# Narrower score and value matmuls in the second block's three attentions

## The chip, the cores and the metric

The kernel runs on one core of one Trainium2 chip. The metric is the device time of one execution in microseconds (us). The engines are TensorE (PE, with its weight loads shown apart as PEld), VectorE (DVE), ScalarE (ACT), GpSimd (POOL) and SyncE (SP, which here only issues DMAs). Each engine runs its own instructions in a fixed order and waits on semaphores for the others.

## The reference

Two transformer blocks of two layers each run one after the other on 256 tokens of 1024 channels, all in fp32. The change touches the second block only, in its token mixer. There a layer has three attentions of 8 heads of 64 channels each, all causal:

```
_swa_sink: dist = i - j;  band = 0 <= dist < 128;  softmax over [logits + bias, sink];  p @ v
_fox:      logits = q.k * scale + c[i] - c[j];     masked where j > i;  softmax;  p @ v
_nsa:      p_c over 15 compressed keys, p_s over selected blocks, p_w over a window, each with
           its own masked softmax; out = g0 * p_c @ vc + g1 * p_s @ v_sel + g2 * p_w @ vw
merged = g_a * (o_a @ w_br_a) + g_b * (o_b @ w_br_b) + g_c * (o_c @ w_br_c);   out = merged @ w_out
```

With 256 tokens in two query tiles of 128, queries 0 to 127 see only keys 0 to 127; queries 128 to 255 see all 256 keys. So of the four (query tile, key tile) squares of a head one is masked as a whole.

## The kernel before, in words

**Numbers.** Every fp32 operand of a matmul is split into two fp32r parts, hi and lo: ScalarE copies hi (`split`, L536; for weights L354), VectorE subtracts to get lo (L537; for weights L356). A product is then three matmuls, hi*hi, hi*lo and lo*hi (`mm3`, L547 to L549). Weights stream from HBM in chunks of 128x1024; each chunk needs one L354 and one L356, and in the projections with 512 columns it feeds 12 matmuls of 512 columns.

**The mixer** is `mix`, called once per layer of the second block. It has three attention phases in a row, each over 8 units (a unit is one head): phase b (`simple` with `prep_b`), phase c (`simple` with `prep_c`, which adds a third score matmul, L1689, for the forget gate), and phase a (the last loop, L1874 on, with compressed, selected and window scores). A unit does this:

- scores on PE: per query tile two matmuls of one q tile against the hi and lo parts of the keys (L1685, L1686; in phase a L1847 for compressed and selected keys together, 32 + 256 columns, and L1851 for the window). In phase b and c both query tiles write into one PSUM bank at columns 0 and 128, 256 columns each, so the second overwrites what the first left of its masked half;
- bias, mask and row minimum on DVE (L625), exponentials on ACT (L615; L1863 in phase a), reciprocal and scaling on DVE (L616, L621; L1868, L1872 in phase a). These read 128 columns for the first query tile and 256 for the second;
- transposes of the three unmasked probability squares on PE (L1710; L1883 and L1884 in phase a), and the split of the 384 columns on ACT and DVE (L536, L537) into the buffers `pts`. Each of these has 512 columns: 128 of zeros, written once per layer (L1652), and behind them the three squares, A (second queries, second keys), B (first queries, first keys) and C (second queries, first keys);
- values on PE: for each of two key tiles one `mm3` of 256 columns. The first key tile reads B and C, the second reads the zeros and A. Phase a does this for selected and window keys and adds one matmul for the compressed keys (L1904).

**What fills in.** Between a unit's steps the code calls `fill(ns)`, which takes pieces of other work from a queue: projections of 512 columns (`natural`), the compression of the keys and, in phase c and a, the gates and branch products of the attention before (`branch_job`). These pieces are `mm3`s of 512 columns, each with its share of weight splits L354 and L356 and of evacuations (L1770, L1787, L1789).

**What sets the order.** When the program is built, a scheduler puts the recorded operations of each engine into one fixed sequence by their priority and by its own estimate of when each can run. Weight splits are moved in priority by `PREP` (L353). Buffers come from two arenas by best fit, so the size of one buffer can move others.

Of the kernel before, what the change touches and what calls it, by code (L numbers as in the profile page):

```python
# [18 lines left out]
P = 128  # L19
D = 1024  # L20
KT = D // P
S = 256
# [456 lines left out]
class Kern:  # L479
# [979 lines left out]
    def mix(self, l, xh, xl, mid):  # L1459
        nc, fa, ra, d = self.nc, self.fa, self.ra, self.d  # L1460
        V, A, G, PE = nc.vector, nc.scalar, nc.gpsimd, nc.tensor
# [17 lines left out]
        def parts(n):  # L1479
            b = ra.alloc(4 * n)  # L1480
            v = b.v("p (z t c) -> p z t c", z=2, t=2)
            return b, v[:, 0], v[:, 1]
# [3 lines left out]
        vswb, vsh, vsl = parts(256)  # L1486
# [22 lines left out]
        pick = pickb.a  # L1509
# [135 lines left out]
        self.push(fill_job())  # L1645

        sr = Ring(fa, 448, 3)
        pts = []
        for i in range(2):
            b = (ra.alloc(512), ra.alloc(512))  # L1650
            for z in b:
                V.tensor_copy(z.a[:, 0:P], self.zero[:, 0:P])  # L1652
            pts.append(b)
        qr = Ring(ra, S, 4)

        def pair_rows(src, c):
# [10 lines left out]
        def pair_out(og, bank, j):  # L1667
            h, lo = og
            c = slice(j * S, j * S + S)
            for k, r in enumerate((slice(0, 64), slice(64, 128))):  # L1670
                self.split(bank[r, k * S:k * S + S], h[r, c], lo[r, c])

        def simple(prep, vh, vl, paired, og, extra):

            units = [(j, i) for j in range(4) for i in range(2)]
            heads = {0: prep(0)}
            prob = {}

            def soft(u):
                j, i = u  # L1680
                q, (kh, kl), b, sink, h = heads[j][i]
                bank = self.ps.next()
                for qt in range(2):
                    qq, o = q[:, qt * P:qt * P + P], bank[:, qt * P:qt * P + S]
                    PE.matmul(o, qq, kh, start=True, stop=False)  # L1685
                    PE.matmul(o, qq, kl, start=False, stop=extra is None)  # L1686
                    if extra:
                        n = P if qt == 0 else S
                        PE.matmul(bank[:, qt * P:qt * P + n], pick[:, h:h + 1].to_broadcast([P, P]), extra[:, 0:n],  # L1689
                                  start=False, stop=True)  # L1690
                sb, ss = sr.next(), self.sm.next()
                w = 0 if sink is None else 1
                for qt in range(2):
                    n = P if qt == 0 else S
                    s = sb[:, 132 * qt:132 * qt + n + 1]
                    m, r = ss[:, 2 * qt:2 * qt + 1], ss[:, 2 * qt + 1:2 * qt + 2]
                    if w:
                        G.tensor_copy(s[:, n:n + 1], sink)
                    self.neg_add_min(s[:, :n], bank[:, qt * P:qt * P + n], b[:, S - n:], sink if w else BIG, m)
                    self.soft_tail(s, n, m, r, n + w)  # L1700
                prob[u] = sb

            for n, u in enumerate(units):
                if n == 0:
                    soft(u)
                j, i = u
                sb = prob.pop(u)
                bank = self.pt.next()
                for k, o in enumerate((132 + P, 0, 132)):
                    PE.transpose(bank[:, k * P:k * P + P], sb[:, o:o + P], ident)  # L1710
                p_h, p_l = pts[n % 2]
                self.split(bank[:, 0:384], p_h.a[:, P:], p_l.a[:, P:])
                if i == 0 and j < 3:
                    heads[j + 1] = prep(j + 1)
                if n + 1 < 8:
                    soft(units[n + 1])
                self.fill(1300)
                if i == 0:
                    self.obank = self.po.next()
                c = slice(j * P, j * P + P) if paired else slice(0, P)  # L1720
                o = self.obank[:, i * S:i * S + S]
                for kt in range(2):
                    r = slice(S - kt * S, 2 * S - kt * S)
                    self.mm3(o, vh[:, kt, c], vl[:, kt, c], p_h.a[:, r], p_l.a[:, r], kt == 0, kt == 1)
                if i == 1:
                    pair_out(og, self.obank, j)
                self.fill(700)
# [15 lines left out]

        ogb, og = new_og()
        simple(prep_b, vbh, vbl, False, og, None)
        self.flush()
        for b in (kwb, vbb, qbb, t5, gf):
# [69 lines left out]
        W1 = 288  # L1817
        slb, wib = ra.alloc(4 * W1), ra.alloc(4 * S)
        sl4 = slb.v("p (i z k) -> p i z k", i=2, z=2)
        wi4 = wib.v("p (i z k) -> p i z k", i=2, z=2)  # L1820
# [20 lines left out]
        def soft(u):  # L1841
            j, i = u
            q, hd = heads[j][i], j + 4 * i
            bs, bw = self.ps.next(), self.ps.next()
            for qt in range(2):
                for z in range(2):
                    PE.matmul(bs[:, 160 * qt:160 * qt + W1], q[:, qt * P:qt * P + P], sl4[:, i, z],  # L1847
                              start=z == 0, stop=z == 1)
            for qt in range(2):
                for z in range(2):  # L1850
                    PE.matmul(bw[:, P * qt:P * qt + S], q[:, qt * P:qt * P + P], wi4[:, i, z],  # L1851
                              start=z == 0, stop=z == 1)
            s1, s2, mm, rr = sr.next(), sr.next(), self.sm.next(), self.sm.next()
            todo = []
            for qt in range(2):
                n = P if qt == 0 else S
                for br, (dst, src, o, w, bias) in enumerate((
                        (s1, bs, 160 * qt, 32, cb4[:, qt, hd]),
                        (s1, bs, 160 * qt + 32, n, t53[:, hd, S - n:]),
                        (s2, bw, P * qt, n, t53[:, hd, S - n:]))):  # L1860
                    c = 3 * qt + br
                    self.neg_add_min(dst[:, o:o + w], src[:, o:o + w], bias, 1e20 if br == 0 else BIG, mm[:, c:c + 1])
                    A.activation(dst[:, o:o + w], dst[:, o:o + w], AF.Exp, bias=mm[:, c:c + 1], scale=-1.0,  # L1863
                                 accum_out=rr[:, c:c + 1])
                    todo.append((dst[:, o:o + w], rr[:, c:c + 1]))
            r6 = rr[:, 0:6]
            V.tensor_scalar(r6, r6, 1e-30, None, ALU.max)
            V.reciprocal(r6, r6)  # L1868
            r3 = r6.rearrange("p (t b) -> p t b", t=2)
            V.tensor_tensor(r3, r3, sg[:, :, 3 * hd:3 * hd + 3], ALU.mult)  # L1870
            for s, r in todo:
                V.tensor_scalar(s, s, r, None, ALU.mult)  # L1872
            prob[u] = (s1, s2)

        soft(units[0])
        for n, u in enumerate(units):
            j, i = u
            s1, s2 = prob.pop(u)
            pc = pcr.next()
            for k, (s, o, w) in enumerate(((s1, 160, 32), (s2, P, 0))):  # L1880
                bank = self.pt.next()
                for kk_, c in enumerate((o + w + P, w, o + w)):
                    PE.transpose(bank[:, kk_ * P:kk_ * P + P], s[:, c:c + P], ident)  # L1883
                PE.transpose(bank[0:32, 384:512], s1[:, 160 * k:160 * k + 32], ident)  # L1884
                self.split(bank[:, 0:384], pts[k][0].a[:, P:], pts[k][1].a[:, P:])
                cq, bq = slice(k * P, k * P + P), bank[0:32, 384:512]
                A.copy(pc[0:32, cq], bq)
                V.tensor_tensor(pc[32:64, cq], bq, pc[0:32, cq].bitcast(F32), ALU.subtract)
                A.copy(pc[64:96, cq], bq)
            if i == 0 and j < 3:  # L1890
                heads[j + 1] = q_pair(qa, j + 1)
            if n + 1 < 8:
                soft(units[n + 1])
            self.fill(2500)
            if i == 0:
                self.obank = self.po.next()
            o = self.obank[:, i * S:i * S + S]
            for k in range(2):
                for kt in range(2):
                    r = slice(S - kt * S, 2 * S - kt * S)  # L1900
                    c = slice(k * P, k * P + P)
                    self.mm3(o, vsh[:, kt, c], vsl[:, kt, c], pts[k][0].a[:, r], pts[k][1].a[:, r],
                             k == 0 and kt == 0, False)
            PE.matmul(o, vcmp.a, pc, start=False, stop=True)  # L1904
            if i == 1:
                pair_out(og_a, self.obank, j)
            self.fill(1000)
# [55 lines left out]
```

## Time and profile before

| what | value |
|---|---|
| time, three runs | 2344.83 us median (2343.74 to 2349.3) |
| the profiled execution | 2346.41 us; its span in the trace 2344.6 us |
| PE busy | 2261.1 us, 96% of the span, 11612 matmuls |
| DVE busy | 1696.6 us, 72% |
| ACT busy | 1249.1 us, 53% |
| mean granted TensorE clock | 0.993 of 2.4 GHz |
| matmuls of mm3, L547 to L549 | 9648 of 11612 |

A matmul's duration in the trace is longer than its share of PE's time, since matmuls overlap: the time from one start to the next is what counts. Phases b, c and a of the first layer run from about 1226 to 1259, 1296 to 1329 and 1356 to 1418 us, those of the second layer from about 1901 to 1934, 1970 to 2004 and 2031 to 2093 us.

### The profile page before, as it was taken

What the parts mean: (1) busy time and instruction counts of PE and PEld (TensorE: products, weight loads), DVE (VectorE), ACT (ScalarE), POOL (GpSimd) and SP (SyncE); (2) the same over time, 40 slices, a digit from 0 to 9 for tenths busy, and PEclk for the clock granted to TensorE, in tenths of its full rate; (3) what the DMA queues carried; (4) which work ended last, traced back from release to release, by engine and by line L of the source; (5) the groups of instructions that cost most, each with busy time, mean ns of one, the idle gap of its engine ahead of it and who ended that gap; (6) DMA issues with size and microseconds to landing.
All of it is one profiled execution on the core that took longest, in us unless ns stands there. A gap on an engine that the chain in (4) does not pass through costs nothing.

```text
span 2344.6 us, 32027 instructions
## 1 busy us (share of the span) xinstructions
PE 2261.1 (96%) x11612; PEld 1858.8 (79%) x11612; DVE 1696.6 (72%) x3192; ACT 1249.1 (53%) x2235; POOL 244.0 (10%) x265
## 2 busy tenths in 40 slices
PE   6999899999999999999999999999999999999998
PEld 3888787787778899888877777788788877777887
DVE  6598999677689997655577897755655677897554
ACT  6385673242347864444367785444444376764452
POOL 1302200222220202200000000000000000000000
PEclk9999999999999999999999999999999999999999
DMA  8121224355443335555646435556556545445554
GB/s 321 45 82 41 75 81 135 126 165 168 134 139 110 103 132 171 179 186 180 220 137 205 138 117 173 179 188 197 189 190 219 163 153 184 144 131 179 189 190 134
DMA packets 102975, 362.98 MB, mean 155 GB/s; under 512 B 11936, under 2 KB 13088, under 8 KB 102304
## 3 DMA queue, kind: packets, MB, share of 16 engines
q1 hardware_dynamic: 102816, 360.93, 46.5%
q8 instruction: 91, 1.49, 0.3%
q14 instruction: 68, 0.56, 0.1%
HBM read 359.84 MB, written 1.05 MB: 154 GB/s over the span
## 4 chain that ended last, share of the span: by engine, by line
PE 55%; DVE 8%; ACT 4%; DMA 3%; issue 2%; POOL 1%; DVEq 0%; ACTq 0%; POOLq 0%; SPq 0%
PE bank L547 17%; PE bank L549 17%; PE bank L548 16%; DVE ra_t L356 2%; ACT ra_t L354 1%; DMA fa_t<-in_gate 1%; PE bank L1402 1%; DVE ra_t L537 1%; DVE fa_t L625 1%; DVE fa_t L1339 1%; DMA fa_t<-in_n 1%; PE bank L1265 1%; ACT ra_t L536 1%; POOL fa_t L543 0%; ACT fa_t L1863 0%
## 5 line engine op out<-in xcount | busy, mean ns | idle before, releaser
L547 PE MATMUL bank<-ra_t 128*128 128x512 f32 (+1 forms) x3216 | 1186.9, 371 | 14.3 <-DVE fa_t L786 5.0
L549 PE MATMUL bank<-ra_t 128*128 128x512 f32 (+1 forms) x3216 | 1172.8, 366 | 8.3 <-DVE ra_t L537 3.8
L548 PE MATMUL bank<-ra_t 128*128 128x512 f32 (+1 forms) x3216 | 1174.6, 367 | 3.8 <-DVE ra_t L537 1.3
L356 DVE TENSOR_TENSOR ra_t<-fa_t,ra_t 128x1024 fp32r<-128x1024 f32 x583 | 722.2, 1241 | 349.1 <-ACT ra_t L354 333.6
L354 ACT CAST ra_t<-fa_t 128x1024 fp32r<-128x1024 f32 x606 | 633.2, 1048 | 602.2 <-PE bank L549 284.5
L547 PEld LDWEIGHTS bank<-ra_t 128*128 128x128 f32 x3216 | 605.4, 189 | 129.1 <-ACT ra_t L536 15.4
L549 PEld LDWEIGHTS bank<-ra_t 128*128 128x128 f32 x3216 | 605.6, 189 | 108.7 <-DVE ra_t L537 7.3
L548 PEld LDWEIGHTS bank<-ra_t 128*128 128x128 f32 x3216 | 607.2, 189 | 103.1 <-DVE ra_t L356 5.1
L865 DVE SCALAR_TENSOR_TENSOR fa_t<-fa_t 128x512 f32<-128x512 f32 (+1 forms) x240 | 161.5, 673 | 6.0 <-ACT fa_t L863 2.8
L537 DVE TENSOR_TENSOR ra_t<-bank,ra_t 128x512 fp32r<-128x512 f32 (+5 forms) x234 | 131.2, 568 | 44.0 <-ACT ra_t L536 41.1
L536 ACT CAST ra_t<-bank 128x512 fp32r<-128x512 f32 (+5 forms) x234 | 112.8, 488 | 84.8 <-PE bank L549 33.4
L543 POOL TENSOR_TENSOR fa_t<-fa_t 128x1 f32<-128x1 f32 (+2 forms) x54 | 69.0, 1278 | 762.3 <-DVE fa_t L542 762.1
L625 DVE CUSTOM_DVE_ANT_0 fa_t<-bank,fa_t 128x256 f32<-128x256 f32 (+2 forms) x320 | 117.0, 396 | 8.7 <-PE bank L1231 1.9
L615 ACT ACTIVATE fa_t<-fa_t 128x257 f32<-128x257 f32 (+5 forms) x160 | 91.5, 574 | 21.4 <-DVE fa_t L625 20.1
L1410 ACT ACTIVATE fa_t<-bank 128x256 f32<-128x256 f32 x88 | 33.9, 385 | 112.5 <-PE bank L549 112.4
L356 POOL TENSOR_TENSOR ra_t<-fa_t,ra_t 128x1024 fp32r<-128x1024 f32 x23 | 58.0, 2520 | 276.1 <-ACT ra_t L354 273.0
L1412 DVE TENSOR_TENSOR fa_t<-fa_t,bank 128x256 f32<-128x256 f32 x88 | 36.8, 418 | 65.7 <-ACT fa_t L1410 65.5
L1184 DVE SCALAR_TENSOR_TENSOR fa_t<-fa_t 128x512 f32<-128x512 f32 x98 | 71.0, 757 | 2.3 <-DMA fa_t<-in_ada 2.0
L1053 POOL TENSOR_TENSOR fa_t<-fa_t 128x512 f32<-128x512 f32 (+1 forms) x32 | 37.3, 1172 | 154.4 <-DVE fa_t L1052 154.4
L638 DVE TENSOR_TENSOR ra_t<-bank,ra_t 64x256 fp32r<-64x256 f32 (+1 forms) x96 | 43.5, 455 | 8.3 <-ACT ra_t L637 5.3
L649 POOL CAST ra_t<-fa_t 64x256 fp32r<-64x256 f32 (+3 forms) x40 | 24.0, 606 | 241.4 <-PE bank L1597 69.9
L1863 ACT ACTIVATE fa_t<-fa_t 128x32 f32<-128x32 f32 (+2 forms) x96 | 39.0, 409 | 14.5 <-DVE fa_t L625 13.9
(218 smaller groups left out, 1701.9 us busy)
## 6 DMA issues: line engine op xcount, KB each, us to landing
fa_t<-in_f1w SPq DMA_DIRECT2D x132, 512.0 KB, 4.2
fa_t<-in_f2w SPq DMA_DIRECT2D x132, 512.0 KB, 4.3
fa_t<-in_tr SPq DMA_DIRECT2D x88, 512.0 KB, 3.5
fa_t<-in_n SPq DMA_DIRECT2D x56, 512.0 KB, 3.6
fa_t<-in_ada SPq DMA_DIRECT2D x48, 512.0 KB, 4.5
fa_t<-in_gate SPq DMA_DIRECT2D x48, 512.0 KB, 3.7
fa_t<-in_nat SPq DMA_DIRECT2D x36, 512.0 KB, 4.2
fa_t<-in_proj SPq DMA_DIRECT2D x24, 512.0 KB, 3.5
```

The lines of the kernel that those rows point to most:

```text
L354: nc.scalar.copy(hi, raw)
L356: eng.tensor_tensor(lo, raw, hi.bitcast(F32), ALU.subtract)
L536: self.nc.scalar.copy(hi, src)
L537: self.nc.vector.tensor_tensor(lo, src, hi.bitcast(F32), ALU.subtract)
L543: self.nc.gpsimd.tensor_tensor(out, out, self.nhalf[:, :n], ALU.pow)
L547: mm(ps, lh, rh, start=start, stop=False)
L548: mm(ps, lh, rl, start=False, stop=False)
L549: mm(ps, ll, rh, start=False, stop=stop)
L615: nc.scalar.activation(s[:, :width or n], s[:, :width or n], AF.Exp, bias=mneg, scale=-1.0, accum_out=r)
L625: self.nc.vector.tensor_tensor_reduce(out=out, in0=a, in1=b, op0=ALU.add, op1=ALU.min, scale=-1.0, scalar=init, accum_out=acc)
L865: V.scalar_tensor_tensor(y4, src, w, y4, ALU.mult, ALU.add)
L1184: V.scalar_tensor_tensor(acc[s].a, wk, self.sc[:, kt, s:s + 1], acc[s].a, ALU.mult, ALU.add)
```

## The change

For the first query tile the score matmuls now take 128 key columns in place of 256 (160 in place of 288 in phase a). The zeros in front of the probabilities are gone: `pts` has 384 columns per buffer, the 8 fills of L1652 (4 per layer) are not there, and the values of the second key tile are made from square A alone, 128 columns, added to the second half of the output. That is 320 matmuls in both layers: 128 of scores (64 in phases b and c, 64 in phase a, of which 32 go from 288 to 160) and 192 of values (96 and 96). No matmul is added or taken away, and all that DVE and ACT read and write in a unit keeps its size.

```
-        pts = []
-        for i in range(2):
-            b = (ra.alloc(512), ra.alloc(512))
-            for z in b:
-                V.tensor_copy(z.a[:, 0:P], self.zero[:, 0:P])
-            pts.append(b)
+        pts = [(ra.alloc(3 * P), ra.alloc(3 * P)) for _ in range(2)]
...
                 for qt in range(2):
-                    qq, o = q[:, qt * P:qt * P + P], bank[:, qt * P:qt * P + S]
-                    PE.matmul(o, qq, kh, start=True, stop=False)
-                    PE.matmul(o, qq, kl, start=False, stop=extra is None)
+                    n = P if qt == 0 else S
+                    qq, o = q[:, qt * P:qt * P + P], bank[:, qt * P:qt * P + n]
+                    PE.matmul(o, qq, kh[:, :n], start=True, stop=False)
+                    PE.matmul(o, qq, kl[:, :n], start=False, stop=extra is None)
                     if extra:
-                        n = P if qt == 0 else S
-                        PE.matmul(bank[:, qt * P:qt * P + n], pick[:, h:h + 1].to_broadcast([P, P]), extra[:, 0:n],
-                                  start=False, stop=True)
+                        PE.matmul(o, pick[:, h:h + 1].to_broadcast([P, P]), extra[:, 0:n], start=False, stop=True)
...
-                self.split(bank[:, 0:384], p_h.a[:, P:], p_l.a[:, P:])
+                self.split(bank[:, 0:384], p_h.a, p_l.a)
...
-                o = self.obank[:, i * S:i * S + S]
-                for kt in range(2):
-                    r = slice(S - kt * S, 2 * S - kt * S)
+                for kt, r in enumerate((slice(P, 3 * P), slice(0, P))):
+                    o = self.obank[:, i * S + kt * P:i * S + S]
                     self.mm3(o, vh[:, kt, c], vl[:, kt, c], p_h.a[:, r], p_l.a[:, r], kt == 0, kt == 1)
...
             for qt in range(2):
+                n = P if qt == 0 else S
                 for z in range(2):
-                    PE.matmul(bs[:, 160 * qt:160 * qt + W1], q[:, qt * P:qt * P + P], sl4[:, i, z],
+                    PE.matmul(bs[:, 160 * qt:160 * qt + 32 + n], q[:, qt * P:qt * P + P], sl4[:, i, z, :32 + n],
                               start=z == 0, stop=z == 1)
...
-                    PE.matmul(bw[:, P * qt:P * qt + S], q[:, qt * P:qt * P + P], wi4[:, i, z],
+                    PE.matmul(bw[:, P * qt:P * qt + n], q[:, qt * P:qt * P + P], wi4[:, i, z, :n],
                               start=z == 0, stop=z == 1)
...
-                for kt in range(2):
-                    r = slice(S - kt * S, 2 * S - kt * S)
+                for kt, r in enumerate((slice(P, 3 * P), slice(0, P))):
                     c = slice(k * P, k * P + P)
-                    self.mm3(o, vsh[:, kt, c], vsl[:, kt, c], pts[k][0].a[:, r], pts[k][1].a[:, r],
+                    self.mm3(o[:, kt * P:], vsh[:, kt, c], vsl[:, kt, c], pts[k][0].a[:, r], pts[k][1].a[:, r],
                              k == 0 and kt == 0, False)
```

The built order changes too. It is the same as before up to the first scores of phase b and from the end of the mixer on, and the same in both layers, but inside a mixer the instructions of PE, DVE and ACT stand otherwise. In the changed kernel the lines of the mixer have numbers that are 4 to 6 lower (L1883 is L1879, L1851 is L1847, L1872 is L1868, L1770 is L1764, L1710 is L1705).

On PE in phase a, before, this is what stands between the window scores of the third unit (L1851) and the transposes of the second (L1883); the rows of bank_65 are fill:

```order
L1851 MATMUL bank_67<-ra_t 128x256 x4
L548 MATMUL bank_65<-ra_t 128x512
L549 MATMUL bank_65<-ra_t 128x512
L547 MATMUL bank_65<-ra_t 128x512
L548 MATMUL bank_65<-ra_t 128x512
L549 MATMUL bank_65<-ra_t 128x512
L547 MATMUL bank_65<-ra_t 128x512
L548 MATMUL bank_65<-ra_t 128x512
L549 MATMUL bank_65<-ra_t 128x512
L547 MATMUL bank_65<-ra_t 128x512
L548 MATMUL bank_65<-ra_t 128x512
L1883 MATMUL bank_68<-fa_t 128x128 x3
```

Now, with L1842 and L1847 for the scores and L1879 for the transposes:

```order
L1842 MATMUL bank_66<-ra_t 128x160 x2
L1842 MATMUL bank_66<-ra_t 128x288 x2
L1847 MATMUL bank_67<-ra_t 128x128 x2
L1879 MATMUL bank_68<-fa_t 128x128 x3
L1880 MATMUL bank_68<-fa_t 32x128
L1847 MATMUL bank_67<-ra_t 128x256
L1879 MATMUL bank_69<-fa_t 128x128 x3
```

The ten matmuls of fill are no longer ahead of these transposes. Counted from the transposes of the first unit to those of the last, phase a has 137 matmuls of 512 columns before and 94 now; phase c has 77 and 60, phase b 66 and 46. What is taken out stands between the phases now (101 and 114 from b to c, 97 and 121 from c to a) or behind the last unit.

On DVE in phase a, before, the rows ahead of the scaling (L1872) of the second unit:

```order
L1888 TENSOR_TENSOR ra_t<-bank_69,ra_t 32x128
L356 TENSOR_TENSOR ra_t<-fa_t,ra_t 128x1024
L1888 TENSOR_TENSOR ra_t<-bank_68,ra_t 32x128
L1867 TENSOR_SCALAR fa_t<-fa_t 128x6
L638 TENSOR_TENSOR ra_t<-bank_69,ra_t 64x256
L1868 RECIPROCAL fa_t<-fa_t 128x6
L1770 TENSOR_TENSOR fa_t<-bank_64,fa_t 128x512
L1870 TENSOR_TENSOR fa_t<-fa_t 128x6
L356 TENSOR_TENSOR ra_t<-fa_t,ra_t 128x1024
L638 TENSOR_TENSOR ra_t<-bank_69,ra_t 64x256
L1872 TENSOR_SCALAR fa_t<-fa_t 128x32
```

Now, with L1884 for L1888 and L1863 to L1868 for L1867 to L1872:

```order
L1884 TENSOR_TENSOR ra_t<-bank_69,ra_t 32x128
L1884 TENSOR_TENSOR ra_t<-bank_68,ra_t 32x128
L625 ISA fa_t<-bank_67,fa_t 128x256
L625 ISA fa_t 128x1
L356 TENSOR_TENSOR ra_t<-fa_t,ra_t 128x1024
L638 TENSOR_TENSOR ra_t<-bank_69,ra_t 64x256
L1863 TENSOR_SCALAR fa_t<-fa_t 128x6
L1864 RECIPROCAL fa_t<-fa_t 128x6
L1866 TENSOR_TENSOR fa_t<-fa_t 128x6
L1868 TENSOR_SCALAR fa_t<-fa_t 128x32
```

One weight split (L356) and one evacuation of fill (L1770) have moved out of this place. Over the same stretch of phase a as above, L356 stands there 12 times before and 9 times now and the evacuation L1789 (now L1783) 4 and 2 times; in phase c L356 6 and 4, L1770 3 and 2 and L625 28 and 26 times, L638 11 and 12; in phase b L356 9 and 7 times. All else of DVE is as often there as before.

## Rows read from the trace of the kernel before

**Rows 1.** The page, part 1: busy time of each engine, share of span.

```profile
PE 2261.1 (96%) x11612; PEld 1858.8 (79%) x11612; DVE 1696.6 (72%) x3192; ACT 1249.1 (53%) x2235; POOL 244.0 (10%) x265
```

**Rows 2.** Busy time by stretch: b, c, between, a; a of layer 1.

```profile
core 0: us, PE busy (x) PEld busy (x) DVE busy (x) ACT busy (x) POOL busy (x), PEclk, DMA share, GB/s
1226.30:1259.30 33.00, 31.86 (x189) 25.77 (x189) 28.89 (x88) 27.33 (x64) 2.70 (x9) 1.00 0.45 146
...
1295.90:1329.50 33.60, 32.69 (x186) 25.83 (x187) 30.90 (x100) 26.01 (x68) 1.86 (x5) 1.00 0.35 113
1329.50:1356.40 26.90, 26.48 (x130) 21.36 (x130) 17.95 (x48) 16.85 (x44) 0.00 (x0) 1.00 0.48 157
1356.40:1418.20 61.80, 59.09 (x339) 47.93 (x338) 58.34 (x199) 46.38 (x145) 6.15 (x4) 1.00 0.37 120
...
2030.90:2092.80 61.90, 59.15 (x340) 48.05 (x339) 58.40 (x199) 46.45 (x146) 6.16 (x4) 1.00 0.38 120
```

**Rows 3.** The chain of waits in phase a: start us, us, what.

```profile
1363.22 1.13 DVE ra_t L356
1364.83 1.30 DVE fa_t L1872 x6
...
1374.62 0.69 DVE fa_t L1872 x3
1375.35 0.55 PE bank L1883 x3
```

**Rows 4.** PE's waits in the first mixer: us in total, times, longest.

```profile
PE bank L1883 <- DVE fa_t L1872: 2.2, 3, 0.9
```

**Rows 5.** Timeline of PE, scores to transposes of phase a: start, us.

```profile
1362.48 0.73 PE L1847 MATMUL bank<-ra_t 128*128 128x288 f32 x4
1363.05 0.63 PE L1851 MATMUL bank<-ra_t 128*128 128x256 f32 x4
1363.52 0.40 PE L548 MATMUL bank<-ra_t 128*128 128x512 f32 x1
...
1365.56 0.39 PE L548 MATMUL bank<-ra_t 128*128 128x512 f32 x1
1365.92 0.55 PE L1883 MATMUL bank<-fa_t 128*128 128x128 f32 x3
```

**Rows 6.** Timeline of PE, scores of one unit of phase c.

```profile
1291.74 0.28 PE L1686 MATMUL bank<-ra_t 128*128 128x256 f32 x1
1291.86 0.22 PE L1689 MATMUL bank<-ra_t 128*128 128x128 f32 x1
1291.92 0.33 PE L1685 MATMUL bank<-ra_t 128*128 128x256 f32 x1
1292.09 0.28 PE L1686 MATMUL bank<-ra_t 128*128 128x256 f32 x1
1292.21 0.28 PE L1689 MATMUL bank<-ra_t 128*128 128x256 f32 x1
1292.32 0.40 PE L548 MATMUL bank<-ra_t 128*128 128x512 f32 x1
```

**Rows 7.** Timeline of the weight loads, the same place.

```profile
1291.74 0.19 PEld L1689 LDWEIGHTS bank<-ra_t 128*128 128x128 f32 x1
1291.86 0.19 PEld L1685 LDWEIGHTS bank<-ra_t 128*128 128x128 f32 x1
1291.97 0.19 PEld L1686 LDWEIGHTS bank<-ra_t 128*128 128x128 f32 x1
```

**Rows 8.** DVE groups in phase a: busy us, mean ns, idle before.

```profile
L356 DVE TENSOR_TENSOR ra_t<-fa_t,ra_t 128x1024 fp32r<-128x1024 f32 x12 | 15.6, 1300 | 0.1
...
L625 DVE CUSTOM_DVE_ANT_0 fa_t<-bank,fa_t 128x128 f32<-128x128 f32 x13 | 3.7, 288 | 0.9 <-PE bank L1884 0.8
...
L1789 DVE SCALAR_TENSOR_TENSOR fa_t<-fa_t,bank 128x512 f32<-128x512 f32 x4 | 2.7, 683 | 0.1
```

**Rows 9.** Line L1652: duration ns min/median/max, first and last start us.

```profile
L1652 DVE CAST ra_t<-fa_t x8: 218/220/221, 1140.9 to 1831.9; 128x128 fp32r<-128x128 f32 x8
```

More of the change, by code (lines that the diff above doesn't have):

```diff
@@ L1845, in soft @@
             for qt in range(2):
+                n = P if qt == 0 else S
                 for z in range(2):
-                    PE.matmul(bs[:, 160 * qt:160 * qt + W1], q[:, qt * P:qt * P + P], sl4[:, i, z],
+                    PE.matmul(bs[:, 160 * qt:160 * qt + 32 + n], q[:, qt * P:qt * P + P], sl4[:, i, z, :32 + n],
                               start=z == 0, stop=z == 1)
             for qt in range(2):
+                n = P if qt == 0 else S
                 for z in range(2):
-                    PE.matmul(bw[:, P * qt:P * qt + S], q[:, qt * P:qt * P + P], wi4[:, i, z],
+                    PE.matmul(bw[:, P * qt:P * qt + n], q[:, qt * P:qt * P + P], wi4[:, i, z, :n],
                               start=z == 0, stop=z == 1)
@@ L1884, in mix @@
                 PE.transpose(bank[0:32, 384:512], s1[:, 160 * k:160 * k + 32], ident)
-                self.split(bank[:, 0:384], pts[k][0].a[:, P:], pts[k][1].a[:, P:])
+                self.split(bank[:, 0:384], pts[k][0].a, pts[k][1].a)
                 cq, bq = slice(k * P, k * P + P), bank[0:32, 384:512]
```

## The prediction

> **What bounds the kernel now.** I read the page's busy shares first, then the busy time by stretch, then the chain of waits and the waits of PE inside one mixer, and last the timelines of single matmuls. Over the whole span PE is busy 96% [rows 1], so outside the mixers less PE work is less time. Inside the three attention phases it is otherwise. In phase a DVE is busy 58.34 of 61.8 us, 94%, in phase c 30.90 of 33.6 and in phase b 28.89 of 33.0, while between the phases, as from c to a, it is busy 17.95 of 26.9 and PE 26.48 [rows 2]. Layer 1 repeats it (58.40 of 61.9 in phase a) [rows 2]. So PE and DVE are both near full in the phases, and only PE between them. The chain of waits in phase a says which leads: it runs through a weight split on DVE and the scalings L1872, and goes to PE at 1375.35 when the last L1872, from 1374.62, lets the transposes L1883 go [rows 3]. PE's own list has that wait on top, 2.2 us in three waits [rows 4]. So PE's fill just about covers the softmax: between the scores and the transposes at 1365.92 PE runs ten fill matmuls and then waits a little, 0.36 us from the last start at 1365.56 where 0.227 would do [rows 5].
>
> **The change, part by part.**
>
> *The narrowed matmuls.* 320 of them go from 256 to 128 columns or from 288 to 160. The pace is the time from start to start. A wide one of 512 columns takes 0.227 us (1363.52 to 1365.56 is nine of them) [rows 5]. One of 256 takes 0.115 (1292.09 to 1292.32 is two) [rows 6]. The trace has 128-column fp32r matmuls already: L1689 of the first query tile. The next matmul starts 0.06 us after it, but the one behind that only 0.17 later, so the pair takes 0.23, as two of 256 columns do [rows 6]. The loads of the weights show why: they start at 1291.74, 1291.86 and 1291.97, one every 0.115 us, whatever the number of columns [rows 7]. Each of these matmuls has its own load, so columns below 256 are hidden behind it. Bounds: nothing at all, and 0.056 us (half of 0.115) for each. I go by the row of the same form, which shows no gain to its rounding of 0.01 us, and take half of that rounding, 0.005 each: 288 x 0.005 = 1.4 us. The 32 of 288 columns stand 0.57 / 4 = 0.143 apart (1362.48 to 1363.05) [rows 5]; down to 0.115 that is 0.9 us. Together 2.3 us less PE work in the kernel, nearly all of it inside the phases.
>
> The Trainium skill has a rule for each end. "TensorE: Matmul & The Clock Gate", section "Back-to-back issue gap", gives N / 2.4 + 2.5 ns at the full clock, so about 56 ns for 128 columns; by it the edit would save some 17 us. The same page's section "LDWEIGHTS (loading the stationary operand)" gives P / 1.2 ns, 107 ns for 128 weight columns; by it nearly nothing is saved. This trace agrees with the second where every matmul loads its own weights.
>
> *The fills of zeros.* 8 casts of 0.22 us on DVE [rows 9], from 1140.9 on, ahead of phase b, in a place where DVE isn't the bound. I take nothing; at most 1.8 us.
>
> *The evacuations, exponentials and splits* keep their sizes, so the softmax of a unit costs DVE and ACT what it did.
>
> *The order.* This is the large term. The scheduler, it seems, counts the narrower matmuls as shorter; it puts the attention's steps earlier among the fill. By the counts in the section on the change, phase b loses 20 wide matmuls of cover, phase c 17 and phase a 43, together 80 x 0.227 = 18.2 us per layer. That work isn't gone. It is done between the phases or behind the last unit, where PE is the bound [rows 2], and costs its 18.2 us there. Minus the 0.2 us of the narrowing that lies outside the stretches, the time outside grows by 18.0 us per layer. What the phases give back is set by DVE. Less fill means fewer weight splits and evacuations in them: 1.30 us for an L356, 0.683 for an L1789, which I use for L1770 too [rows 8].
>
> - phase b: 2 L356, 2.6 us: 28.9 to 26.3 us of DVE
> - phase c: 2 L356 and 1 L1770, 3.3 us: 30.9 to 27.6 (two L625 less and one L638 more I take as even)
> - phase a: 3 L356 and 2 L1789, 5.3 us: 58.3 to 53.0
>
> DVE needs 106.9 us after, where the three stretches now last 33.0 + 33.6 + 61.8 = 128.4 us with 118.1 of DVE and 10.3 us of DVE idle. How much of that idle time stays decides:
>
> - all 10.3 us: the stretches last 117.2, 11.2 less, against 18.0 more outside: +6.8 per layer, +13.6 in all
> - three quarters, 7.7 us: 13.8 less, +4.2 per layer, +8.4 in all
> - half: 16.3 less, +1.7 per layer, +3.4
> - none: 21.5 less, -3.5 per layer, -7.0
>
> I take three quarters. Of 3.5 us idle in phase a 0.8 was DVE's waiting for PE [rows 8], a quarter, which should go when PE comes to the transposes with time to spare. The rest is the way through ACT and the semaphores, which the change leaves alone. The narrowing inside the phases is in this already, since DVE sets their length; so is what PE gains by it.
>
> *The sum.* +8.4 us on the profiled execution's 2346.4 us gives 2354.8. The median of the runs is 1.6 us lower, 2344.8, and what I predict is a median: 2353.
>
> **The rivals.**
>
> *The phases run faster than DVE's idle time suggests (not slower).* With fewer fill matmuls in front of them the transposes and scores are reached at once, and DVE's gaps close. The point from which it decides is 128.4 - 18.0 - 106.9 = 3.5 us of idle time per layer, a third of today's. Below that the change is no loss, and with none left it comes to 2338. For it: PE had waits of only 2.2 us at the transposes [rows 4], so in most units it came no earlier than DVE was ready, and part of the length is PE's. Against it: DVE is at 94% in phase a already [rows 2], and with fewer L356 there is less to fill its gaps with. Its time is 2338 to 2345, say 2342.
>
> *Columns count after all (faster).* If in rows of several narrow matmuls the loads run ahead far enough, each would take half of 0.115 us, 17 to 18 us less PE work; all of it on the path, that is 2327. Against it stands the pair of L1689 and L1685 [rows 6], and that DVE, not PE, is the bound in the phases.
>
> *DVE's idle time grows (slower yet).* The splits and evacuations that filled its gaps are fewer, and the chain from scores over exponentials to scaling is as long as before. With half as much again, 15.5 us, the stretches shrink by 6.0 only: +12 per layer, 2369. For it: the chain in phase a is one of handovers [rows 3]. Against it: all 10.3 us may hold already what that chain needs.
>
> **How the numbers follow.** The forecast, DVE setting the phases with more than a third of its idle time kept, has 0.60; its own range is 2345 to 2358. The closing of the gaps has 0.26, columns 0.06, more idle time 0.08. A measurement of this kernel can tell about 0.3%, 7 us, from no change. Of the forecast 0.42 lies above +7 us (idle time of about seven tenths and more), 0.18 below; with 0.08 of the last rival slower has 0.50. Faster has 0.05 of the columns and 0.02 of the gaps that close wholly, 0.07. The rest, 0.43, is no change. The range of 8 in 10 is 2340 to 2364: it takes in nearly all of the first rival, and leaves out columns, most of the last rival, and little of the forecast.
>
> **What would show it.** In the profile after, a narrowed score matmul must still be followed at a pace of 0.11 us. Phase a must take 54 to 57 us from the first transposes to the last ones (61.8 now), phase c 28 to 31, phase b 28 to 31, with DVE busy 53, 28 and 26 us in them, and PE must wait for the scaling in front of the transposes (L1879 for L1868) in most units, 6 us or more in a mixer instead of 2.2. The stretch from c to a must last about 5 us longer, with PE full. The prediction is wrong if phase a comes down to 52 us or less, if narrow matmuls in a row start 0.06 us apart, or if PE's waits in the mixers stay where they are.

## The result and the profile after

The changed kernel takes 2373.12 us (median of 4 runs, 2372.25 to 2375.07), the kernel before in the same call 2345.32 us: ratio 1.0117, 95% interval 1.01 to 1.0135. It is slower by 27.8 us, where 8 had been predicted. The profiled execution has a span of 2370.4 us (2344.6 before).

Part 1 of the page, to be held against [rows 1]:

```profile
PE 2262.5 (95%) x11612; PEld 1857.2 (78%) x11612; DVE 1697.7 (72%) x3184; ACT 1247.4 (53%) x2235; POOL 246.6 (10%) x265
```

No engine's busy time grew by more than 2.6 us; nearly all of the added time is waiting. TensorE's clock has no visible part in it: the mean granted clock is 0.994 of 2.4 GHz, before 0.993, and 1.00 in every row below. Busy time by stretch, answering [rows 2]: phases b and c, c to a, a, and a of layer 1.

```profile
core 0: us, PE busy (x) PEld busy (x) DVE busy (x) ACT busy (x) POOL busy (x), PEclk, DMA share, GB/s
1225.50:1257.10 31.60, 28.18 (x167) 21.61 (x167) 27.10 (x86) 24.88 (x61) 2.54 (x9) 1.00 0.43 137
...
1296.50:1329.10 32.60, 29.38 (x170) 22.94 (x171) 28.76 (x95) 23.61 (x65) 1.87 (x5) 1.00 0.27 89
1329.10:1361.80 32.70, 31.88 (x154) 25.81 (x152) 21.99 (x52) 21.12 (x48) 0.00 (x0) 1.00 0.49 170
1361.80:1419.50 57.70, 49.01 (x295) 39.86 (x295) 52.67 (x194) 43.57 (x143) 3.47 (x2) 1.00 0.33 104
...
2049.00:2106.80 57.80, 49.07 (x295) 39.94 (x296) 52.78 (x194) 43.65 (x143) 3.46 (x2) 1.00 0.33 105
```

The phases got shorter by only 1.4, 1.0 and 4.1 us, 6.5 together. DVE is busy 108.5 us in them, and 13.4 idle (10.3 before). Phase a now leaves both engines idle: PE 8.7 of 57.7 us, DVE 5.0. The work taken out of the phases stands where it was expected: c to a is 5.8 us longer. From layer 0's first transposes to layer 1's it is 687.4 us, 12.4 more than before.

The chain of waits in phase a (start us, us, what), answering [rows 3]:

```profile
1381.05 1.13 DVE ra_t L356
1382.21 0.43 DVE ra_t L638
1382.85 0.56 DVE fa_t L1783
1383.44 0.44 DVE ra_t L638
1383.90 0.91 DVE fa_t L1866
1385.04 0.40 DVE fa_t L1868 x3
1385.50 0.76 DVE fa_t L1868 x3
```

DVE does one unit's softmax steps (from L1863 at 1380.89, too short for this list, to L1868) with a weight split, an evacuation and two splits of other work among them. PE has run out of fill and waits 1.24 us for the fifth of these six scalings; the sixth belongs to the next transposes. The last score matmuls of the same unit, and its first transposes, on PE:

```profile
1374.47 0.62 PE L1847 MATMUL bank<-ra_t 128*128 128x128 f32 x4
1386.05 0.55 PE L1879 MATMUL bank<-fa_t 128*128 128x128 f32 x3 [1.24 <-DVE fa_t L1868]
```

PE's waits in the first mixer, answering [rows 4]:

```profile
PE bank L1879 <- DVE fa_t L1868: 6.3, 6, 2.6
PE bank L1705 <- DVE fa_t L621: 3.2, 5, 1.4
PE bank L1899 <- ACT ra_t L1885: 1.6, 2, 0.9
```

What DVE waits for in phase a, first before, then after:

```profile
DVE fa_t L625 <- PE bank L1884: 0.8, 2, 0.5
DVE fa_t L625 <- PE bank L1847: 0.2, 1, 0.2
DVE ra_t L1888 <- ACT ra_t L1887: 0.2, 1, 0.2
```

```profile
DVE ra_t L356 <- ACT ra_t L354: 1.0, 2, 0.6
DVE ra_t L537 <- ACT ra_t L536: 0.9, 3, 0.4
DVE fa_t L1863 <- ACT fa_t L1859: 0.9, 2, 0.6
```

DVE's waits for PE are gone, as predicted. Three us of waits for ACT have come in their place (a fourth line, of 0.2 us, is left out).

DVE's weight splits in phase a, answering [rows 8]: nine instead of twelve, as counted.

```profile
L356 DVE TENSOR_TENSOR ra_t<-fa_t,ra_t 128x1024 fp32r<-128x1024 f32 x9 | 11.0, 1220 | 1.0 <-ACT ra_t L354 1.0
```

The narrowed matmuls, answering [rows 6]: PE's timeline of one product with the values (start, us).

```profile
1318.13 0.28 PE L549 MATMUL bank<-ra_t 128*128 128x256 f32 x1
1318.25 0.22 PE L547 MATMUL bank<-ra_t 128*128 128x128 f32 x1
1318.31 0.28 PE L548 MATMUL bank<-ra_t 128*128 128x128 f32 x1
1318.42 0.28 PE L549 MATMUL bank<-ra_t 128*128 128x128 f32 x1
1318.53 0.52 PE L1705 MATMUL bank<-fa_t 128*128 128x128 f32 x3
```

After a matmul of 128 columns the next starts 0.06 us later once (1318.25 to 1318.31), then the pace is 0.11 again. The weight loads keep their pace throughout: they start at 1318.13, 1318.25 and 1318.36.

A place in phase c where the fill is missing:

```profile
1322.38 0.23 PE L1682 MATMUL bank<-ra_t 128*128 128x128 f32 x1
1322.44 0.27 PE L1683 MATMUL bank<-ra_t 128*128 128x128 f32 x1
1324.10 0.55 PE L1705 MATMUL bank<-fa_t 128*128 128x128 f32 x3 [1.39 <-DVE fa_t L621]
1324.40 0.31 PE L1685 MATMUL bank<-ra_t 128*128 128x128 f32 x1
```

Two score matmuls of the next unit are issued. Then PE waits 1.39 us at the transposes of this unit, and the next unit's other scores stand behind them. DVE has a gap of 0.43 us just after, up to 1324.80; by the profile it waits there for ACT (L536), not for PE.

### The profile page after: what moved, and what is told of

Its sections match the earlier page's. It is cut to its first block, busy times and chain, and to the rows that moved or that the text cites. A ratio compares the mean times of both kernels' runs of the same rounds, so it can differ in the third digit from the quotient of the medians.

```text
span 2370.4 us, 32051 instructions
## 1 busy us (share of the span) xinstructions
PE 2262.5 (95%) x11612; PEld 1857.2 (78%) x11612; DVE 1697.7 (72%) x3184; ACT 1247.4 (53%) x2235; POOL 246.6 (10%) x265
## 4 chain that ended last, share of the span: by engine, by line
PE 49%; DVE 13%; ACT 5%; issue 3%; DMA 3%; POOL 1%; DVEq 0%; ACTq 0%; POOLq 0%
PE bank L547 15%; PE bank L549 15%; PE bank L548 15%; DVE ra_t L356 3%; ACT ra_t L354 2%; DVE ra_t L537 1%; DVE fa_t L625 1%; DVE ra_t L638 1%; PE bank L1402 1%; DVE fa_t L865 1%; ACT fa_t L1859 1%; DVE fa_t L1868 1%; DVE fa_t L621 1%; DVE fa_t L1339 1%; DMA fa_t<-in_gate 1%
## 5 line engine op out<-in xcount | busy, mean ns | idle before, releaser
L549 PE MATMUL bank<-ra_t 128*128 128x512 f32 (+1 forms) x3216 | 1174.1, 366 | 9.1 <-DVE ra_t L537 3.8
L356 DVE TENSOR_TENSOR ra_t<-fa_t,ra_t 128x1024 fp32r<-128x1024 f32 x583 | 721.2, 1239 | 368.4 <-ACT ra_t L354 352.4
L549 PEld LDWEIGHTS bank<-ra_t 128*128 128x128 f32 x3216 | 606.1, 189 | 111.3 <-DVE ra_t L537 7.3
L537 DVE TENSOR_TENSOR ra_t<-bank,ra_t 128x512 fp32r<-128x512 f32 (+5 forms) x234 | 130.8, 566 | 42.3 <-ACT ra_t L536 40.2
L536 ACT CAST ra_t<-bank 128x512 fp32r<-128x512 f32 (+5 forms) x234 | 112.8, 487 | 80.3 <-PE bank L549 27.5
L625 DVE CUSTOM_DVE_ANT_0 fa_t<-bank,fa_t 128x256 f32<-128x256 f32 (+2 forms) x320 | 116.1, 394 | 7.2 <-PE bank L1231 1.9
L356 POOL TENSOR_TENSOR ra_t<-fa_t,ra_t 128x1024 fp32r<-128x1024 f32 x23 | 58.0, 2520 | 277.4 <-ACT ra_t L354 254.9
L638 DVE TENSOR_TENSOR ra_t<-bank,ra_t 64x256 fp32r<-64x256 f32 (+1 forms) x96 | 43.5, 455 | 8.5 <-ACT ra_t L637 5.7
L637 ACT CAST ra_t<-bank 64x256 fp32r<-64x256 f32 (+1 forms) x96 | 37.4, 393 | 15.9 <-DVE ra_t L638 6.6
```

What stands on the lines that cost most here:

```text
L356: eng.tensor_tensor(lo, raw, hi.bitcast(F32), ALU.subtract)
L536: self.nc.scalar.copy(hi, src)
L537: self.nc.vector.tensor_tensor(lo, src, hi.bitcast(F32), ALU.subtract)
L549: mm(ps, ll, rh, start=False, stop=stop)
L625: self.nc.vector.tensor_tensor_reduce(out=out, in0=a, in1=b, op0=ALU.add, op1=ALU.min, scale=-1.0, scalar=init, accum_out=acc)
```

## The experiments

Sixteen kernels separate the narrowing from the order, and then ask what in the order counts. "Before" is 2345 to 2348 us in every call.

### Order or matmuls

To hold an order, a table of the wanted sequence is turned into dependencies without a wait between neighbours on each engine:

```diff
+def in_order(nc, tc, engines=None):
+    for e, text in ORDER.items():
...
+        for a, b in zip(at, at[1:]):
+            tc.add_manual_dep(here[b], here[a].name, why, reason="order")
```

**e1_narrow_old_order**: the changed kernel in the old sequence (probability buffers of 512 columns, of which 384 are used).

> All the narrowed matmuls of the change and none of the fills of zeros, but every engine issues its instructions in the sequence of the kernel before (66, 101, 77, 97 and 137 wide matmuls in phase b, b to c, c, c to a and a, instead of 46, 114, 60, 121 and 94). Theory, the loss is the order: the time goes back to that of the kernel before less the 2 us of the narrowing, 2340 to 2346 us, and PE waits about 2 us in a mixer at the scaling as before. Rival, the narrow matmuls (or the missing fills of zeros) cost the time themselves: it stays at 2370 to 2375 us.

**e2_wide_new_order**: the kernel before in the new sequence (its eight fills of zeros left free).

> The kernel before, with every matmul as wide as it was and the fills of zeros, in the sequence of the changed kernel on every engine. Theory, the order: 2373 to 2377 us, with phase a at 58 us and c to a at 33 us, as in the changed kernel. Rival, the narrow matmuls themselves: 2345 us. If both hold in part, the sum of this run's and of the first run's distance from the kernel before is the 28 us of the change.

Measured: 2343.37 us (ratio 0.999, 0.998 to 0.9999) and 2371.61 us (1.0116, 1.0092 to 1.0139). Phase a of e1, and c to a and a of e2, columns as above:

```profile
1353.60:1415.50 61.90, 58.65 (x340) 47.39 (x339) 58.50 (x199) 46.36 (x146) 6.14 (x4) 1.00 0.37 120
```

```profile
1334.60:1367.20 32.60, 31.89 (x153) 25.90 (x151) 21.90 (x52) 21.02 (x48) 0.00 (x0) 1.00 0.51 170
1367.20:1425.00 57.80, 49.69 (x295) 40.41 (x295) 52.78 (x194) 43.66 (x143) 3.48 (x2) 1.00 0.33 103
```

The order makes the whole loss: wide matmuls in the new sequence have the changed kernel's phases, narrow ones in the old sequence have the old phases. The narrowing, together with the missing fills of zeros, saves some 2.6 us in this pair of kernels. e1 is also the only version whose interval lies below the kernel before, by 0.1%.

### The two halves alone

**e3_scores_only** takes from the change the narrow scores alone, **e4_values_only** the narrow values and the missing zero tile alone. Some of the lines that each puts back into the changed kernel:

```diff
# e4: scores as before
+                    qq, o = q[:, qt * P:qt * P + P], bank[:, qt * P:qt * P + S]
+                    PE.matmul(o, qq, kh, start=True, stop=False)
...
# e3: values as before, with the zero tile
+                for kt in range(2):
+                    r = slice(S - kt * S, 2 * S - kt * S)
...
```

> Only the score matmuls are narrowed; values and zero tile as before; the scheduler sets the order: 59, 101, 60, 121 and 109 wide matmuls, so 52 less in the phases of a layer than before instead of 80. Theory, the order, if each wide matmul that leaves a phase costs the same (28 us for 2 x 80): 52 / 80 of it, +18 us, 2363 us (2358 to 2368). Rival, each of the two halves costs by what it does itself: half or less of 28 us, however the counts are, +14 us or less.

> Only the matmuls of probabilities with values are narrowed and the zero tile is gone; the scores are as wide as before; the scheduler sets the order: 49, 112, 58, 122 and 108 wide matmuls, 65 less in the phases of a layer. Theory, the order, at the same cost for each: 65 / 80 of 28 us, +23 us, 2368 us (2362 to 2372). Both halves together then come to +41 us, more than the whole change. Rival, the matmuls themselves: both halves add up to 28 us.

Measured: 2356.59 us (+10.6) and 2358.47 us (+12.5). Both expectations were too high, and the sum, 23, is near the whole change's 28, as the rival had it; the rival's reason, a cost of the matmuls themselves, is excluded by e1. The count of wide matmuls in the phases does not set the price.

### Count or cover

What I then looked at is the PE work between a unit's last score matmul and its transposes, its cover, counted at 0.227 us for a matmul of 512 columns, 0.143 for 288 and 0.115 for the others.

```diff
# e5: phase a; e6: all phases
-            self.fill(2500)
+            self.fill(3500)    # e6: 5000
-            self.fill(1000)
+            self.fill(1400)    # e6: 2000
# e6, phases b and c
-                self.fill(1300)
+                self.fill(2600)
-                self.fill(700)
+                self.fill(1400)
# e7: as e6, and in both kinds of phase
+                    with self.tc.high_priority(offset=60):
+                        soft(units[n + 1])
```

> The changed kernel with more fill called for in phase a: 3500 and 1400 ns a unit instead of 2500 and 1000. Phase a then holds 130 wide matmuls instead of 94, but the scheduler puts the new ones ahead of a unit's scores; between the last score matmul and the transposes of the same unit stand as many us of PE work as in the changed kernel (phase a: 4.3 8.3 5.3 9.0 7.7 8.0 3.8 6.2 us; changed kernel 4.3 8.3 4.6 8.5 7.6 7.5 5.7 6.2; kernel before 4.6 11.5 10.1 12.1 8.1 10.7 9.7 10.9). Theory, what counts is the work that covers a unit's softmax: nothing comes back, 2370 to 2375 us, and phase a gets about 8 us longer per layer. Rival, what counts is the number of wide matmuls in the phase, at 27.8 / 160 = 0.17 us each: 2 x 36 x 0.17 = 12.5 us less, 2361 us.

> The changed kernel with twice the fill in every phase: 91, 70, 110, 70 and 134 wide matmuls, 335 in the phases (before 280, changed 200). Phase b is covered better than before, phase c about as well, phase a worse (4.3 8.3 8.0 10.0 9.8 5.1 6.0 5.7 us). Theory, cover, with what a softmax needs taken as 4.6 us in b and c and 10.5 us in a: missing cover per layer is 16.2 us before, 45.4 changed, here 32.8, so (32.8 - 16.2) / (45.4 - 16.2) of the 27.8 us stay: 2361 us (2356 to 2366). Rival, the number of wide matmuls: more than before, so at or below it, 2345 us or less.

> As the run with twice the fill, and the next unit's scores and softmax get a higher priority, so that the scheduler puts fill behind them instead of ahead: 91, 70, 94, 82 and 144 wide matmuls, 329 in the phases, nearly the same number, but more of them between scores and transposes (missing cover 23.2 us per layer). Theory, cover: 2352 us (2347 to 2357), some 9 us less than the run with twice the fill alone. Rival, the number: the same time as that run within 3 us.

Measured: e5 2369.85 us (1.0095, 1.008 to 1.011), e6 2364.50 (1.0073, 1.0058 to 1.0088), e7 2357.87 (1.0044, 1.0027 to 1.0061). Phase a of e5:

```profile
1361.50:1426.50 65.00, 56.04 (x332) 46.46 (x332) 57.71 (x199) 46.50 (x145) 5.12 (x4) 1.00 0.38 122
```

36 more wide matmuls (8.2 us) made the phase 7.3 us longer: fill that stands ahead of the scores gives little back (3 us less than the changed kernel, where the count would give 12.5). With 329 and 335 wide matmuls in the phases, more than the 280 of before, e7 and e6 are still slower than before; the 6.6 us between them came with the better cover of e7. Count is refuted; cover orders these three as expected (e7 0.9 us above its range, e5 0.15 below). It is no more than a rough measure: the sum of missing cover by which e6 was priced, taken from the traces of e3 and e4, gives +16 and +13 us (an estimate), where +10.6 and +12.5 were measured.

### A shorter way through ACT

**e8_no_sums**: the changed kernel's own sequence on PE, DVE and ACT, without the row sums of the exponentials (POOL sets the sums to 1). Phase a is shown; phases b and c leave them out likewise.

```diff
-                    A.activation(dst[:, o:o + w], dst[:, o:o + w], AF.Exp, bias=mm[:, c:c + 1], scale=-1.0,
-                                 accum_out=rr[:, c:c + 1])
+                    A.activation(dst[:, o:o + w], dst[:, o:o + w], AF.Exp, bias=mm[:, c:c + 1], scale=-1.0)
```

> The changed kernel in its own sequence on PE, DVE and ACT, but the exponentials of the second block's attentions leave out their row sums (the sums are taken as 1). DVE's work and PE's work stay; ACT's part of a unit's way from scores to transposes gets shorter by some 0.3 us in phases b and c and 0.7 us in phase a (0.1 us for each exponential behind another, 0.19 for the last read of a sum). Theory, the way of one unit from its scores over DVE and ACT back to PE sets the phases: they shrink, by up to 8 x (0.3 + 0.3 + 0.7) = 10.4 us per layer and by about half of it if half of the units wait for it: 2363 us (2356 to 2368). Rival, DVE's busy time with a fixed idle time between its instructions sets the phases: 2371 to 2373 us.

Measured: 2365.53 us (1.008, 1.0065 to 1.0095), 7.6 us less than the changed kernel, within the theory's range. Phase a:

```profile
1360.40:1416.80 56.40, 48.95 (x297) 39.89 (x296) 52.25 (x194) 40.07 (x105) 4.95 (x11) 1.00 0.33 104
```

In the changed kernel ACT is busy only 43.6 of 57.7 us in phase a, so time on ACT was on the path as latency. It does not settle all: the phases of layer 0 shrank by 3.2 us, and half of it is DVE's own busy time, which was meant to stay (108.5 to 106.9). The other half is idle time (13.4 to 11.8).

### Which engine's sequence

**e9 to e14, e16 and e17.** Here the old sequence is held on some engines and the scheduler sets the others around it. e14, e13 and e16 hold the same engines as e9, e11 and e17, with the probability buffers of 512 columns that e1 has.

```diff
+        in_order(nc, tc, ('PE',))                         # e9
+        in_order(nc, tc, ('DVE', 'Activation'))           # e10
+        in_order(nc, tc, ('PE', 'DVE'))                   # e11
+        in_order(nc, tc, ('PE', 'Activation'))            # e12
+        in_order(nc, tc, ('PE', 'DVE', 'Activation'))     # e17
```

> The changed kernel, with its own small buffers, where only PE is held to the sequence of the kernel before; the scheduler sets the sequence of DVE, ACT, POOL and SP anew around it. Theory, PE's sequence decides, since it holds the work between a unit's scores and its transposes: 2340 to 2348 us, as with all engines held. Rival, the sequence on DVE and ACT matters as much: some 10 us above that, 2353 us or more.

> The reverse of the run before: the changed kernel, with DVE and ACT held to the sequence of the kernel before, and PE's sequence left to the scheduler. PE's comes out near the old one by itself: 67, 102, 74, 98 and 134 wide matmuls, 18.7 us of missing cover per layer (kernel before 16.2, changed kernel 45.4). Theory, a unit's steps must stand at the same places on PE, DVE and ACT, and PE's cover must match them: both hold nearly, 2344 to 2352 us. Rival, any sequence that is not the old one on all engines costs some 25 us: 2365 us or more. If it is at 2345 us or less, the sequence on DVE and ACT alone decided.

> The changed kernel with PE and DVE held to the sequence of the kernel before, the others left to the scheduler. Holding PE alone gave 2375 us, holding DVE and ACT 2366 us, holding all 2343 us. Theory, PE and DVE are the pair that has to match, since DVE does most of a unit's steps: 2343 to 2350 us. Rival, ACT's sequence (its splits of the probabilities, for which PE waited 6.2 us in ten waits when PE alone was held) is as sensitive: 2355 us or more.

> The changed kernel with PE and ACT held to the sequence of the kernel before, DVE left to the scheduler. Theory, PE and DVE are the pair that has to match: it stays well above the kernel before, 2355 to 2370 us. Rival, ACT's splits alone were late when only PE was held: 2343 to 2350 us.

Measured: 2374.66, 2365.96, 2371.07 and 2371.06 us. My theory fell in e9, e10 and e11 (e12 came out 1 us above its range): with the old sequence, and so the old cover, on PE alone the loss is all there, and DVE with it is not enough. Phase a of e10, where DVE and ACT keep the old sequence:

```profile
1359.10:1425.70 66.60, 59.90 (x335) 46.75 (x335) 58.14 (x199) 46.70 (x146) 6.30 (x4) 1.00 0.34 112
```

DVE has the same work in the same sequence as before (58.1 us, 58.3 before), and the phase takes 66.6 us instead of 61.8. e1 differed in its buffers too, so that was asked next:

> The changed kernel with probability buffers of 512 columns, and PE, DVE and ACT held to the sequence of the kernel before (POOL and SP free). Both theories: 2341 to 2347 us, as with all five engines held; if not, POOL's or SP's sequence carries the loss.

> The same three engines held to the old sequence, but with the changed kernel's buffers of 384 columns. Theory A, the sequences of PE, DVE and ACT must all match and the buffers don't matter: 2341 to 2347 us. Theory B, the smaller buffers move others and bring waits that the old sequence doesn't suit: 2360 to 2375 us, as with two engines held.

> PE and DVE held, buffers of 512 columns. Theory A: 2371 us, as with 384 columns. Theory B: 2343 to 2350 us.

> PE alone held, buffers of 512 columns. Theory A: 2375 us, as with 384 columns. Theory B: 2343 to 2355 us.

Measured: e16 2344.51 us (0.9993, 0.9984 to 1.0003), e17 2345.45 (0.9996, 0.9987 to 1.0006), e13 2374.81, e14 2380.08. With the three old sequences held together the old time comes back, whichever the buffers (e16 and e17 are 0.9 us apart). With one or two held, and the rest as this scheduler then sets it, it doesn't. Other sequences for the free engines were not tried, so it is not shown that no other would fit. There the larger buffers are slower too: e13 by 3.7 us than e11 and e14 by 5.4 than e9, with the same sequences on PE, DVE and ACT; but for the clock, the reason stays open.

The granted clock is part of the loss in some of these runs. Inside the two mixers of the profiled runs it stands at 1.2 GHz for 23.8 us in e12, 20.4 in e14 and 10.2 in e9, for 3.4 in the changed kernel, and not at all in e10, e16 and e17. In e12 PE had been busy 6.1 of the 9.7 us before the first such stretch, which starts at 1250.7. At half of 2.4 GHz such a stretch can lose at most half of its length: by this estimate up to 12 us of e12's 25.5, and up to 5 of the 5.4 between e14 and e9.

How an engine with a new sequence holds up the others is in the waits of DVE in the first mixer, in e1 and then in e11, where of these three ACT alone is free (L538 and L539 are L536 and L537 of the kernel before):

```profile
DVE ra_t L539 <- ACT ra_t L538: 5.0, 9, 1.3
```

```profile
DVE ra_t L539 <- ACT ra_t L538: 17.9, 21, 1.9
```

In e11 the scheduler put some hi parts of splits later on ACT than e1 has them, those of the probabilities by up to six places, while DVE's sequence is fixed. DVE stands at L539 with its other work behind it, and PE waits at the values (L549, the first matmul of a product, here of 256 columns):

```profile
PE bank L549 <- ACT ra_t L538: 6.0, 10, 1.0
```

In e9 that line reads 6.2 us. In the kernel before PE waited 0.5 us for the same split. The changed kernel itself doesn't show this: DVE waits there 3.8 us, in six waits, for the hi parts. So e11 shows one way in which sequences can fail to fit, but hardly the one that costs the 28 us.

## Why the prediction was wrong

- **The order, and what it costs outside: right.** 18.0 us per layer were predicted. Measured are 12.4 + 6.5 = 18.9: the layer's growth and what the three phases gave back. e1, e2 and e17 show that nothing else in the change costs time.
- **The narrowing: right.** 2.3 us less PE work; e1, e16 and e17, all with narrow matmuls and without the fills of zeros in the old sequence, are 2.6, 1.7 and 0.8 us below the kernel before, and only e1's interval is clear of no change. The pace stays at 0.11. The 17 us that the prediction worked out from the Trainium skill, "TensorE: Matmul & The Clock Gate", section "Back-to-back issue gap", rest on a formula that this section itself gives for an isolated matmul and calls too low for few columns, since it leaves out the weight load.
- **DVE's work in the phases: nearly right**, 106.9 us predicted, 108.5 measured; phase b gave back 1.8 us instead of 2.6 and phase c 2.1 instead of 3.3.
- **DVE's idle time: this step failed.** I let three quarters of 10.3 us remain, 7.7, because its waits for PE should go. They went, but 13.4 us are idle now. In phase a it is 5.0 us (3.5 before), and 3.0 of them are waits for ACT. With DVE's 1.6 us more it makes the stretches 6.5 us shorter instead of 13.8, and that is 7.3 us per layer, 15 in all, of the 19 by which the forecast is too low. The rival in which idle time grows, with a chance of 0.08, had 15.5 us, +12 per layer and 2369; it names what happened. Its reason, that with fewer fillers the chain from scores over exponentials to scaling shows, fits: e8 made ACT's part of that chain shorter and won 7.6 us. That the missing fillers are the whole cause is not shown, since in e11 PE and DVE have all of the old fill in the old places, and the kernel loses 26 us.
- **Behind it is the premise that DVE at 94% sets a phase's length.** e10 speaks against it: the same work of DVE in the same sequence takes 4.8 us longer in phase a. Each engine goes through its fixed sequence, and they hand each unit round between them, so I read the share near one as the effect of fill that fitted, not as a sign of one engine as the bound. The time between the start of a unit's last score matmul and its transposes fits that. In the changed kernel's phase a it is 10.6 to 11.2 us in four of the eight units, while PE has 7.5 to 8.5 us of work to put there; the old sequence had 10.1 to 12.1 us of work there in five.
- **Of the signs:** phase a 57.7 us (54 to 57 predicted), c 32.6 and b 31.6 (28 to 31), all above; PE's wait for L1868 6.3 us in six (6 or more), c to a 5.8 longer (about 5), DVE 53, 29, 27 (53, 28, 26): as said.

Open stays what in the sequences decides, beyond that they must fit. Cover explains e5 to e7, where the scheduler planned all engines together, but not e10, whose cover is near the old one and which is 18 us slower, nor e9, e11 and e12, whose cover is the old one.

## What to carry to other kernels

Where a scheduler's estimates set a fixed order, a change that makes instructions shorter on paper is first a change of the order: compare the sequences, and price what is taken out of a stretch of handovers at its full duration, with only a part coming back (here 6.5 of 18.9 us per layer). Two engines that are busy 94% and 96% over such a stretch are not a proof that one of them bounds it. If an edit is wanted and its new order is not, hold the old order on every engine that hands work round: holding one or two of three, with the rest left to the scheduler, cost 18 to 34 us here.

## What the runs showed of the hardware

DVE's softmax instructions of six columns take 0.15 to 0.19 us, but six of them in the two traces take 0.81 to 0.92, and each of the six lies beside an addition of 512 columns on POOL. POOL and then DVE in phase a of the changed kernel:

```profile
1383.49 1.29 POOL L1784 TENSOR_TENSOR fa_t<-fa_t 128x512 f32<-128x512 f32 x1 [57.75 <-DVE fa_t L1783]
```

```profile
1383.90 0.91 DVE L1866 TENSOR_TENSOR fa_t<-fa_t 128x6 f32<-128x6 f32 x1
1384.84 0.19 DVE L625 CUSTOM_DVE_ANT_0 fa_t<-bank,fa_t 128x32 f32<-128x32 f32 x1
```

L1866 ends at 1384.81, POOL at 1384.78. Not every such instruction is held up: two reciprocals of the kernel before (L1868, 0.18 us) lie beside an addition and are not, and there a weight split behind them takes 2.21 us instead of 1.22. The Trainium skill, "SBUF — State Buffer", section "Who interferes with whom", says that a DVE instruction with two SBUF inputs, or in a two-port mode, contends with a GpSimd instruction that reads SBUF, and that the one that issues first keeps the shared ports for its whole instruction. L1866 has two inputs in SBUF, and the common end agrees with it; whether L1863, L1867 and L1872, with one, run in such a mode no run shows. In phase a the kernel before loses more by it than the changed one, some 2.8 us against 1.4 per layer (an estimate from these durations and an L1872 of 1.38 us instead of 0.28), so it explains nothing of the 28 us.
